# The last four granules of a down projection as one group beside the closing norms, and a sigmoid that stays in its PSUM bank

## The chip, the cores and the metric

The kernel runs on one core of one Trainium2 chip. Its time is the device time of one execution in microseconds; a kernel's time is the median of several executions. PE is the matmul engine, PEld its weight load, DVE, ACT and POOL the three other compute engines, SP the engine on whose queue all the DMAs here are issued.

## The reference

Two blocks on 1024 tokens of 1024 features. The first is a gated mix of attention and convolution, then a two-layer MLP, then a gated product. Only the end of the first block matters here:

```python
h = rms_norm(x, g_pre_mlp[i])
f = jnp.square(jax.nn.relu(h @ w_up[i])) @ w_down[i]
x = x + rms_norm(f, g_post_mlp[i])

ple_gate = jax.nn.sigmoid(rms_norm(x, g_ple[i]) @ w_ple_gate[i])
x = x + ple_gate * (p[i] @ w_ple_proj[i])
```

The hidden width of the MLP is 4096, so the down projection sums over 32 pieces of 128 rows, called granules below. The second block begins with `rms_norm_2(x, norm_pre[0])` and projections of the result.

## The kernel before

All matmuls are done in three passes, because each fp32 operand is split into a high part and a rest: `mm3` (L119) issues high by high (L124), high by rest (L125) and rest by high (L126) for each 128 rows of the sum. A weight is loaded by `split_w` (L90): a DMA into one of two raw buffers (L103), the high part on ACT (L104), the rest on POOL (L105). The two parts go into slots of the pools `w` and `wx`, six slots in all, taken in turn, unless `room` names another pool.

`mlp` keeps the whole result of the down projection in SBUF (`acc`, 8 token tiles by 1024). `down(js)` takes a group of granules: for each token tile t and each half n of the features it sums the group's granules in one PSUM bank (`ps_d`, one of six banks of the tag r) and adds the bank to `acc` on DVE (L1037). There are 16 groups of two granules, so a group has 8 x 2 x 2 x 3 = 96 matmuls and 16 additions to `acc`.

Beside the last group, granules 30 and 31, `after(t)` does the closing work of the token tiles that are complete:

- `final(t)` (L996 to L1017) squares and sums `acc` for tile t and, once the residual is added, for tile t - 1 (L1004 on ACT). Each sum becomes a reciprocal root on DVE in about ten tiny steps (`rstd`, L144 to L163). Tile t is then multiplied by the gain (L1007 on POOL, L1008 on DVE), scaled (L1012 on ACT) and added to the residual `x_f` (L1013 on POOL, L1014 on DVE), and `normed(t - 1)` writes the normed row tile `xn` (L989 on DVE for one half; L991 on ACT and L992 on POOL for the other).
- `turn(t - 3)` transposes `xn` on PE (L183, eight 128x128 transposes into two banks `tp`) and splits it (L112 on ACT, L113 on DVE) into `act_hi` and `act_lo`.
- `ple(n, t - 4)` multiplies by half n of the gate weight (24 matmuls into `ps_pg`), takes the sigmoid on ACT into the SBUF tile `g_p` (L1050), multiplies it by `pp_t` on DVE (L1051) and adds the product to `acc` on POOL (L1052).

After the group, the gate's second half `w1` is loaded (L1069) and `ple(1, t)` runs with the next norm (`leave`) and its transposes. Then come gates of the next layer (`ps_g`, `ps_ad`), whose weights take their slots in the same turn.

In the normed rows, tile 3 has a buffer of its own in the pool `fp` (`xn_f`), and the first two pieces of `w1` lie in that pool too. The order of each engine's instructions is set when the program is built, by a scheduler that works from the program's dependences; on the chip every engine goes through its list in order.

Of the kernel before, what the change touches and what calls it, by code (L numbers as in the profile page):

```python
# [8 lines left out]
F32 = mybir.dt.float32  # L9
# [3 lines left out]
AF = mybir.ActivationFunctionType  # L13
ALU = mybir.AluOpType
# [4 lines left out]
P = 128  # L19
S = 1024  # L20
D = 1024
# [7 lines left out]
class Net:  # L29
# [914 lines left out]
    def mlp(self):  # L944


        nc, tc, a = self.nc, self.tc, self.a
# [4 lines left out]
        with ExitStack() as st:  # L952
# [6 lines left out]
            fp = st.enter_context(tc.tile_pool(name="fp", bufs=2))  # L959
# [3 lines left out]
            f3 = st.enter_context(tc.tile_pool(name="f3", bufs=2))  # L963
            acc = ac.tile([P, NT, D], F32, name="acc")

            def gain(src):
                g = gl.tile([P, D], F32, name="gain", tag="gain")
                nc.sync.dma_start(out=g, in_=src.broadcast_to([P, D]))
                return g

            def load_f(j):

                s = (j + 4) % 8
                fs[j] = hi[:, s, :], lo[:, s, :]
                for h in range(2):
                    sl = slice(h * H, h * H + H)
                    raw = fr.tile([P, H], F32, name="f_raw")
                    nc.sync.dma_start(out=raw, in_=self.fd[j, :, sl])
                    self.split(*(x[:, sl] for x in fs[j]), raw)

            gp, gn = gain(a["g_post_mlp"]), gain(a["g_ple"])

            def normed(t, q, g):
                if t == 3 and g is gn:
                    o = xn[t] = fp.tile([P, D], F32, name="xn_f", tag="fh")
                else:
                    o = xn[t] = f3.tile([P, D], F32, name="xn", bufs=3)
                x = acc[:, t, :]
                nc.vector.scalar_tensor_tensor(out=o[:, :H], in0=x[:, :H], scalar=q, in1=g[:, :H],  # L989
                                               op0=ALU.mult, op1=ALU.mult)  # L990
                nc.scalar.activation(out=o[:, H:], in_=x[:, H:], func=AF.Copy, scale=q)  # L991
                nc.gpsimd.tensor_tensor(out=o[:, H:], in0=o[:, H:], in1=g[:, H:], op=ALU.mult)  # L992
# [3 lines left out]
            def final(t):  # L996

                if t < NT:
                    x = f3.tile([P, D], F32, name="x_f", bufs=1)
                    nc.sync.dma_start(out=x, in_=self.xd[t * P:(t + 1) * P, :])  # L1000
                    a0, a1 = acc[:, t, :H], acc[:, t, H:]
                    ss = self.sm.tile([P, 2 if t else 1], F32, name="ss")
                    for i in range(2 if t else 1):
                        nc.scalar.activation(out=junk(), in_=acc[:, t - i, :], func=AF.Square, accum_out=ss[:, i:i + 1])  # L1004
                    qs = self.rstd(ss, D)
                    q1, q = qs[:, 0:1], qs[:, 1:2] if t else None
                    nc.gpsimd.tensor_tensor(out=a0, in0=a0, in1=gp[:, :H], op=ALU.mult)  # L1007
                    nc.vector.tensor_tensor(out=a1, in0=a1, in1=gp[:, H:], op=ALU.mult)  # L1008
                else:
                    q = self.rstd(self.sumsq(acc[:, t - 1, :], junk()), D)  # L1010
                if t < NT:
                    nc.scalar.activation(out=a0, in_=a0, func=AF.Copy, scale=q1)  # L1012
                    nc.gpsimd.tensor_tensor(out=a0, in0=a0, in1=x[:, :H], op=ALU.add)  # L1013
                    nc.vector.scalar_tensor_tensor(out=a1, in0=a1, scalar=q1, in1=x[:, H:], op0=ALU.mult, op1=ALU.add)  # L1014
                if t:
                    normed(t - 1, q, gn)

            xn = {}

            def turn(t):  # L1020
                self.transpose_split(xn[t], pst, t, hi, lo, 8, 0)

            def down(js, after=None):
                ws = [self.split_w(a["w_down"][j], 1024) for j in js]
                for j in js:
                    load_f(j)
                for t in range(NT):
                    ts = slice(t * P, (t + 1) * P)
                    for n in range(2):
                        sl = slice(n * H, n * H + H)  # L1030
                        ps = psm.tile([P, H], F32, name="ps_d", tag="r")
                        self.mm3(ps, [((fs[j][0][:, ts], fs[j][1][:, ts]), (w[0][:, sl], w[1][:, sl]))
                                      for j, w in zip(js, ws)])
                        if js[0] == 0:
                            nc.vector.tensor_copy(out=acc[:, t, sl], in_=ps)
                        else:
                            nc.vector.tensor_tensor(out=acc[:, t, sl], in0=ps, in1=acc[:, t, sl], op=ALU.add)  # L1037
                    if after is not None:
                        after(t)

            def ple(n, t, ws):
                ts = slice(t * P, (t + 1) * P)
                sl = slice(n * H, n * H + H)
                ps = psm.tile([P, H], F32, name="ps_pg", tag="r")
                self.mm3(ps, [((hi[:, k, ts], lo[:, k, ts]),
                               tuple(w[:, (k % 2) * H:(k % 2) * H + H] for w in ws[k // 2])) for k in range(8)])
                g = f2.tile([P, H], F32, name="g_p", tag="rl")
                pp = f3.tile([P, H], F32, name="pp_t", bufs=1)
                nc.sync.dma_start(out=pp, in_=self.pp[ts, sl])
                nc.scalar.activation(out=g, in_=ps, func=AF.Sigmoid)  # L1050
                nc.vector.tensor_tensor(out=g, in0=g, in1=pp, op=ALU.mult)  # L1051
                nc.gpsimd.tensor_tensor(out=acc[:, t, sl], in0=acc[:, t, sl], in1=g, op=ALU.add)  # L1052

            for c in range(0, 30, 2):
                down([c, c + 1])
            wg = []

            def after(t):
                final(t)
                if t == 0:  # L1060
                    wg.extend(self.split_w(a["w_ple_gate"][0, k], 1024) for k in range(4))
                if t > 2:
                    turn(t - 3)
                if t > 3:
                    ple(0, t - 4, wg)

            down([30, 31], after)
            g0 = gain(a["norm_pre_2"][0:1])
            w1 = [self.split_w(a["w_ple_gate"][1, k], 1024, room=(fp, "fh", "fl") if k < 2 else None) for k in range(4)]  # L1069

            def leave(t):
                if t < NT:
                    ple(1, t, w1)
                    nc.sync.dma_start(out=self.xd[t * P:(t + 1) * P, :], in_=acc[:, t, :])
                if t:
                    normed(t - 1, self.rstd(self.sumsq(acc[:, t - 1, :], junk()), D), g0)

            final(NT)
            turn(NT - 3)
            ple(0, NT - 4, wg)  # L1080
            turn(NT - 2)
            ple(0, NT - 3, wg)
# [13 lines left out]
            for m in range(2):  # L1096
                ps = psm.tile([P, H], F32, name="ps_g", tag="r")
                self.proj_T(ps, self.g01[m], col, act, 8, 0)
                g = f2.tile([P, H], F32, name="g_p", tag="rl")
# [566 lines left out]
```

## Time and profile before

| what | us |
|---|---|
| three executions | 2941.45, 2939.25, 2936.12 |
| median | 2939.25 |
| the profiled execution | 2939.78 |
| its span, first to last instruction | 2938.0 |

The span is cut into busy time by engine and into stretches (windows). A wait is the idle time of an engine with what ended it. In a timeline the bracket behind a row gives the idle time before that row. PE's own rows overlap, since matmuls are pipelined: a 128x512 matmul shows 0.39 us and the next begins 0.23 us later. [...]

### The profile page before, as it was taken

Reading aid. Unit: us, or ns where it says so; the run is one execution under the profiler, and the core shown is the slowest. Engines: PE = TensorE matmul, PEld = TensorE weight load, DVE = VectorE, ACT = ScalarE, POOL = GpSimd, SP = SyncE. Lnnn points to the kernel's source line nnn. Section 1 sums busy time; section 2 is a strip of 40 time slices with the busy share of each in tenths; the row PEclk is TensorE's granted clock in tenths of the full one; section 3 lists DMA queues with packets and bytes.
Section 4 is the critical chain, followed back from the end, with each engine's and each line's share of the span. In section 5 each row is a group of like instructions: output and inputs, shape, how many; then the busy total and the mean of one; then the engine's idle time right before and its main releaser. Section 6 shows DMA issues by size and latency. Waiting matters only on the chain. (4 is left out here: it accounts for less than half of the span.)

```text
span 2938.0 us, 37990 instructions
## 1 busy us (share of the span) xinstructions
PE 2767.0 (94%) x13490; PEld 2303.1 (78%) x13490; DVE 1684.0 (57%) x3177; ACT 1222.8 (42%) x2403; POOL 985.6 (34%) x826
## 2 busy tenths in 40 slices
PE   7999999997999999999989899699999999999988
PEld 5888778886887887888867789677777988788867
DVE  5420288855387766766577534377872436666643
ACT  5111266643352222211134423377773535555542
POOL 4211111113235543222246312332324344555441
PEclk9999999998999999999999999899999999999999
DMA  5112211117323335332123321543344332222163
GB/s 208 47 43 68 75 46 60 58 61 251 118 97 106 128 109 170 115 105 93 66 71 136 133 94 64 180 122 95 121 137 170 106 117 65 72 72 74 56 204 118
DMA packets 140293, 311.15 MB, mean 106 GB/s; under 512 B 15868, under 2 KB 35964, under 8 KB 140104
## 3 DMA queue, kind: packets, MB, share of 16 engines
q1 hardware_dynamic: 140104, 308.73, 31.4%
q8 instruction: 107, 1.75, 0.2%
q14 instruction: 82, 0.67, 0.1%
HBM read 213.33 MB, written 85.38 MB: 102 GB/s over the span
## 5 line engine op out<-in xcount | busy, mean ns | idle before, releaser
L105 POOL TENSOR_TENSOR w_lo<-w_raw,w_hi 128x1024 fp32r<-128x1024 f32 (+5 forms) x223 | 440.2, 1983 | 1036.0 <-ACT w_hi L104 1021.5
L104 ACT ACTIVATE w_hi<-w_raw 128x1024 fp32r<-128x1024 f32 (+5 forms) x223 | 193.0, 877 | 407.3 <-PE ps L125 90.6
L124 PE MATMUL ps_m<-act_hi,w_hi 128*128 128x512 f32 x716 | 287.2, 401 | 22.6 <-DVE qb L343 6.3
L125 PE MATMUL ps_m<-act_lo,w_hi 128*128 128x512 f32 x716 | 281.4, 393 | 0.0
L126 PE MATMUL ps_m<-act_hi,w_lo 128*128 128x512 f32 x716 | 280.7, 393 | 0.2
L113 DVE TENSOR_TENSOR pl<-tp_at,ph 128x512 fp32r<-128x512 f32 (+3 forms) x416 | 222.9, 561 | 84.0 <-ACT ph L112 81.8
L112 ACT ACTIVATE ph<-tp_at 128x512 fp32r<-128x512 f32 (+3 forms) x416 | 196.7, 500 | 107.6 <-PE tp_at L304 96.4
L304 PE MATMUL tp_at<-ident,p 128*128 128x128 f32 x1280 | 204.9, 275 | 18.0 <-DVE pl L113 6.5
L259 ACT ACTIVATE p<-p,mx 128x256 f32<-128x256 f32 (+7 forms) x256 | 180.2, 706 | 74.5 <-DVE mx L248 41.6
L1037 DVE TENSOR_TENSOR acc<-ps_d,acc 128x512 f32<-128x512 f32 x240 | 161.5, 687 | 82.1 <-PE ps_d L126 82.1
L124 PE MATMUL ps_d<-w_hi,act_hi 128*128 128x512 f32 x512 | 200.3, 391 | 2.8 <-DVE f_out L890 1.3
L125 PE MATMUL ps_d<-w_lo,act_hi 128*128 128x512 f32 x512 | 199.5, 390 | 0.0
L126 PE MATMUL ps_d<-w_hi,act_lo 128*128 128x512 f32 x512 | 199.5, 390 | 0.0
L304 PEld LDWEIGHTS tp_at<-ident,p 128*128 128x128 f32 x1280 | 152.6, 141 | 50.6 <-DVE pl L113 9.2
L124 PEld LDWEIGHTS ps_m<-act_hi,w_hi 128*128 128x128 f32 x716 | 135.3, 189 | 58.3 <-PE s_ps L226 8.8
L760 PE MATMUL r_o<-w_hi,act_hi 128*128 128x512 f32 x384 | 152.0, 399 | 12.4 <-DVE ga L692 8.0
L126 PEld LDWEIGHTS ps_m<-act_hi,w_lo 128*128 128x128 f32 x716 | 134.7, 188 | 29.3 <-POOL w_lo L105 1.3
L125 PEld LDWEIGHTS ps_m<-act_lo,w_hi 128*128 128x128 f32 x716 | 135.3, 189 | 25.5
L296 PE MATMUL o_ps<-ph,v 128*128 128x512 f32 (+3 forms) x400 | 146.5, 367 | 6.3 <-ACT ph L112 3.3
L762 PE MATMUL r_o<-w_hi,act_lo 128*128 128x512 f32 x384 | 151.9, 396 | 0.0
L761 PE MATMUL r_o<-w_lo,act_hi 128*128 128x512 f32 x384 | 151.6, 396 | 0.0
L297 PE MATMUL o_ps<-pl,v 128*128 128x512 f32 (+3 forms) x400 | 147.6, 377 | 0.4 <-DVE pl L113 0.2
(393 smaller groups left out, 6930.1 us busy)
## 6 DMA issues: line engine op xcount, KB each, us to landing
w_raw<-in_w_in SPq DMA_DIRECT2D x40, 512.0 KB, 3.5
w_raw<-in_w_up SPq DMA_DIRECT2D x32, 512.0 KB, 3.6
f_rows_up<-f_out SPq DMA_DIRECT2D x64, 256.0 KB, 2.4
f_raw<-f_rows_up SPq DMA_DIRECT2D x64, 256.0 KB, 2.6
w_raw<-in_w_down SPq DMA_DIRECT2D x32, 512.0 KB, 4.5
xd<-x_o SPq DMA_DIRECT2D x16, 512.0 KB, 2.8
x_o<-xd SPq DMA_DIRECT2D x16, 512.0 KB, 10.6
w_raw<-in_w_out SPq DMA_DIRECT2D x13, 512.0 KB, 5.2
```

Of the source, the lines that this page charges most:

```text
L104: nc.scalar.activation(out=hi[:, sl], in_=raw, func=AF.Copy)
L105: nc.gpsimd.tensor_tensor(out=lo[:, sl], in0=raw, in1=hi[:, sl].bitcast(F32), op=ALU.subtract)
L112: nc.scalar.activation(out=hi, in_=src, func=AF.Copy)
L113: nc.vector.tensor_tensor(out=lo, in0=src, in1=hi.bitcast(F32), op=ALU.subtract)
L124: nc.tensor.matmul(out, lhsT=sh, rhs=mh, start=(i == 0), stop=False)
L125: nc.tensor.matmul(out, lhsT=sh, rhs=ml, start=False, stop=False)
L126: nc.tensor.matmul(out, lhsT=sl, rhs=mh, start=False, stop=(i == n - 1))
L259: nc.scalar.activation(out=p[:, :nk], in_=p[:, :nk], func=AF.Exp, scale=-1.0, bias=mx[:, 0:1], accum_out=it["sum"][:, j:j + 1])
L304: nc.tensor.transpose(tp[:, j * P:(j + 1) * P], it["p"][j][:, k * P:(k + 1) * P], self.ident)
L760: nc.tensor.matmul(r, lhsT=a, rhs=wh, start=(k == 0), stop=False)
L762: nc.tensor.matmul(r, lhsT=b, rhs=wh, start=False, stop=(k == 7))
L1037: nc.vector.tensor_tensor(out=acc[:, t, sl], in0=ps, in1=acc[:, t, sl], op=ALU.add)
```

## The change

The last four granules, 28 to 31, form one group of 192 matmuls, so a bank sums four granules and `acc` is added to once for the four. The first two pieces of the gate's first half stay in the six slots and the other two go to the pool `fp`; all four pieces of `w1` go to the six slots. Tile 3's normed rows use the common three buffers. The sigmoid writes its own PSUM bank, and DVE reads that bank. Lines behind L984 move up by three, behind L1066 by two.

```diff
             def normed(t, q, g):
-                if t == 3 and g is gn:
-                    o = xn[t] = fp.tile([P, D], F32, name="xn_f", tag="fh")
-                else:
-                    o = xn[t] = f3.tile([P, D], F32, name="xn", bufs=3)
+                o = xn[t] = f3.tile([P, D], F32, name="xn", bufs=3)
...
-                nc.scalar.activation(out=g, in_=ps, func=AF.Sigmoid)
-                nc.vector.tensor_tensor(out=g, in0=g, in1=pp, op=ALU.mult)
+                nc.scalar.activation(out=ps, in_=ps, func=AF.Sigmoid)
+                nc.vector.tensor_tensor(out=g, in0=ps, in1=pp, op=ALU.mult)
...
-            for c in range(0, 30, 2):
+            for c in range(0, 28, 2):
...
-                    wg.extend(self.split_w(a["w_ple_gate"][0, k], 1024) for k in range(4))
+                    wg.extend(self.split_w(a["w_ple_gate"][0, k], 1024, room=(fp, "fh", "fl") if k > 1 else None)
+                              for k in range(4))
...
-            down([30, 31], after)
+            down([28, 29, 30, 31], after)
...
-            w1 = [self.split_w(a["w_ple_gate"][1, k], 1024, room=(fp, "fh", "fl") if k < 2 else None) for k in range(4)]
+            w1 = [self.split_w(a["w_ple_gate"][1, k], 1024) for k in range(4)]
```

On PE, the place of the first transposes (`tp_...`, of tile 0) among the down projection's matmuls. Before, they stand behind the matmuls of tile 4 in the last group of two (96 + 60 `ps_d` matmuls behind the start of granule 28):

```order
L124 MATMUL ps_d_11623<-w_hi_11371,act_hi_83 128x512
L125 MATMUL ps_d_11623<-w_lo_11372,act_hi_83 128x512
L126 MATMUL ps_d_11623<-w_hi_11371,act_lo_84 128x512
L183 MATMUL tp_11601<-ident_63,xn_11501 128x128 x4
L183 MATMUL tp_11608<-ident_63,xn_11501 128x128 x4
L124 MATMUL ps_pg_11677<-w_hi_11433,act_hi_83 128x512
```

Now they stand inside the last bank of tile 4 of the group of four, 118 matmuls behind that start:

```order
L124 MATMUL ps_d_11549<-w_hi_11227,act_hi_83 128x512
L183 MATMUL tp_11521<-ident_63,xn_11397 128x128 x4
L125 MATMUL ps_d_11549<-w_lo_11228,act_hi_83 128x512
L126 MATMUL ps_d_11549<-w_hi_11227,act_lo_84 128x512
L183 MATMUL tp_11528<-ident_63,xn_11397 128x128 x4
L124 MATMUL ps_pg_11609<-w_hi_11317,act_hi_83 128x512
```

All of the tile's own matmuls moved in front of the first gate matmul in both; what changed is that tiles 0 to 4 bring 120 matmuls of one group, where they brought 60.

On POOL, the pieces of `w1` (`w_lo_...` of L105) among the norms. Before, from tile 4's L1013 on, four pieces (the first stands two rows ahead of this place):

```order
L1013 TENSOR_TENSOR acc_9020<-acc_9020,x_f_11724 128x512
L992 TENSOR_TENSOR xn_11752<-xn_11752,gain_9023 128x512
L105 TENSOR_TENSOR w_lo_11996<-w_raw_11997,w_hi_11995 128x1024
L105 TENSOR_TENSOR w_lo_12002<-w_raw_12003,w_hi_12001 128x1024
L1052 TENSOR_TENSOR acc_9020<-acc_9020,g_p_11888 128x512
L1007 TENSOR_TENSOR acc_9020<-acc_9020,gain_9021 128x512
L105 TENSOR_TENSOR w_lo_12008<-w_raw_12009,w_hi_12007 128x1024
L1013 TENSOR_TENSOR acc_9020<-acc_9020,x_f_11817 128x512
```

Now, from tile 6's L1010 (the L1013 of before) on:

```order
L1010 TENSOR_TENSOR acc_9020<-acc_9020,x_f_11773 128x512
L989 TENSOR_TENSOR xn_11801<-xn_11801,gain_9023 128x512
L105 TENSOR_TENSOR w_lo_11958<-w_raw_11959,w_hi_11957 128x1024
L105 TENSOR_TENSOR w_lo_11964<-w_raw_11965,w_hi_11963 128x1024
L1004 TENSOR_TENSOR acc_9020<-acc_9020,gain_9021 128x512
L105 TENSOR_TENSOR w_lo_11970<-w_raw_11971,w_hi_11969 128x1024
L1010 TENSOR_TENSOR acc_9020<-acc_9020,x_f_11878 128x512
L989 TENSOR_TENSOR xn_11906<-xn_11906,gain_9023 128x512
L1049 TENSOR_TENSOR acc_9020<-acc_9020,g_p_11949 128x512
L105 TENSOR_TENSOR w_lo_11976<-w_raw_11977,w_hi_11975 128x1024
```

The four pieces moved behind tile 6's norm: the first three now stand between the normed rows of tiles 5 and 6.

On POOL again, the end of the stage: the rests of the weights for the next layer's gates among the last normed rows. Before, two stand beside the last two additions to `acc`:

```order
L1052 TENSOR_TENSOR acc_9020<-acc_9020,g_p_12578 128x512
L105 TENSOR_TENSOR w_lo_13078<-w_raw_13079,w_hi_13077 128x1024
L1052 TENSOR_TENSOR acc_9020<-acc_9020,g_p_12645 128x512
L105 TENSOR_TENSOR w_lo_13084<-w_raw_13085,w_hi_13083 128x1024
L992 TENSOR_TENSOR xn_12669<-xn_12669,gain_11987 128x512
L992 TENSOR_TENSOR xn_12704<-xn_12704,gain_11987 128x512
```

Now four stand there:

```order
L1049 TENSOR_TENSOR acc_9020<-acc_9020,g_p_12546 128x512
L105 TENSOR_TENSOR w_lo_12922<-w_raw_12923,w_hi_12921 128x1024
L989 TENSOR_TENSOR xn_12570<-xn_12570,gain_11955 128x512
L105 TENSOR_TENSOR w_lo_12928<-w_raw_12929,w_hi_12927 128x1024
L1049 TENSOR_TENSOR acc_9020<-acc_9020,g_p_12613 128x512
L105 TENSOR_TENSOR w_lo_13046<-w_raw_13047,w_hi_13045 128x1024
L989 TENSOR_TENSOR xn_12637<-xn_12637,gain_11955 128x512
L105 TENSOR_TENSOR w_lo_13052<-w_raw_13053,w_hi_13051 128x1024
L989 TENSOR_TENSOR xn_12672<-xn_12672,gain_11955 128x512
```

Two of the four next-layer pieces that stood earlier in the stage moved to its end, since their slots now hold `w1` until the last gate product.

## Rows read from the trace of the kernel before

**Rows 1.** The page's first part: each engine's busy time, share of the span and instructions.

```profile
PE 2767.0 (94%) x13490; PEld 2303.1 (78%) x13490; DVE 1684.0 (57%) x3177; ACT 1222.8 (42%) x2403; POOL 985.6 (34%) x826
```

**Rows 2.** Windows: bounds, length, busy of PE, PEld, DVE, ACT, POOL, clock, DMA, GB/s.

```profile
1440.00:1475.60 35.60, 35.60 (x159) 29.48 (x158) 17.99 (x26) 3.79 (x4) 9.53 (x4) 1.00 0.18 60
1497.48:1566.00 68.52, 50.93 (x216) 40.25 (x217) 58.27 (x118) 36.11 (x60) 44.19 (x27) 0.85 0.31 108
1566.00:1638.90 72.90, 72.19 (x348) 59.23 (x347) 49.31 (x122) 34.39 (x57) 38.98 (x26) 1.00 0.33 122
1638.90:1651.00 12.10, 8.12 (x36) 6.14 (x34) 8.62 (x19) 7.02 (x11) 5.36 (x4) 0.86 0.37 141
```

**Rows 3.** Waits of PE, 1490 to 1660: line, releaser, total us, times, longest.

```profile
PE tp L183 <- DVE act_lo L113: 11.1, 6, 5.8
PE tp L183 <- DVE xn L989: 7.0, 1, 7.0
PE ps_pg L126 <- DVE act_lo L113: 2.6, 2, 2.2
```

**Rows 4.** Timeline of PE: start us, us, line, operation, idle before and releaser.

```profile
1461.96 0.39 PE L124 MATMUL ps_d<-w_hi,act_hi 128*128 128x512 f32 x1
...
1497.09 0.39 PE L126 MATMUL ps_d<-w_hi,act_lo 128*128 128x512 f32 x1
1504.43 1.08 PE L183 MATMUL tp<-ident,xn 128*128 128x128 f32 x4 [6.95 <-DVE xn L989]
...
1516.55 0.60 PE L183 MATMUL tp<-ident,xn 128*128 128x128 f32 x4
1516.90 0.48 PE L125 MATMUL ps_pg<-w_lo,act_hi 128*128 128x512 f32 x1
...
1543.75 1.12 PE L183 MATMUL tp<-ident,xn 128*128 128x128 f32 x4 [5.83 <-DVE act_lo L113]
...
1557.86 0.78 PE L126 MATMUL ps_pg<-w_hi,act_lo 128*128 128x512 f32 x1 [2.19 <-DVE act_lo L113]
```

**Rows 5.** Timeline of DVE: start us, us, line, operation, idle before and releaser.

```profile
1486.64 0.69 DVE L1037 TENSOR_TENSOR acc<-ps_d,acc 128x512 f32<-128x512 f32 x1 [0.67 <-PE ps_d L126]
...
1503.54 0.75 DVE L989 SCALAR_TENSOR_TENSOR xn<-acc,rstd_y,gain 128x512 f32<-128x512 f32 x1
...
1520.40 0.75 DVE L989 SCALAR_TENSOR_TENSOR xn<-acc,rstd_y,gain 128x512 f32<-128x512 f32 x1
...
1542.35 0.75 DVE L989 SCALAR_TENSOR_TENSOR xn<-acc,rstd_y,gain 128x512 f32<-128x512 f32 x1
...
1548.40 2.31 DVE L153 TENSOR_SCALAR rstd_y<-rstd_x 128x2 int32<-128x2 int32 x1
...
1558.58 0.75 DVE L989 SCALAR_TENSOR_TENSOR xn<-acc,rstd_y,gain 128x512 f32<-128x512 f32 x1
```

**Rows 6.** Timeline of POOL.

```profile
1505.37 1.27 POOL L992 TENSOR_TENSOR xn<-xn,gain 128x512 f32<-128x512 f32 x1
...
1545.45 5.24 POOL L105 TENSOR_TENSOR w_lo<-w_raw,w_hi 128x1024 fp32r<-128x1024 f32 x2
...
1553.14 2.39 POOL L105 TENSOR_TENSOR w_lo<-w_raw,w_hi 128x1024 fp32r<-128x1024 f32 x1
```

**Rows 7.** Lines and tiles: duration in ns, least, median and most.

```profile
L1037 DVE TENSOR_TENSOR acc<-ps_d,acc x240: 674/691/692, 1183.6 to 1544.8; 128x512 f32<-128x512 f32 x120
...
L1008 DVE TENSOR_TENSOR acc<-acc,gain x8: 678/688/1073, 1488.7 to 1555.5; 128x512 f32<-128x512 f32 x8
...
L1051 DVE TENSOR_TENSOR g_p<-g_p,pp_t x16: 679/693/2827, 1523.0 to 1637.3; 128x512 f32<-128x512 f32 x16
...
L113 DVE TENSOR_TENSOR act_lo<-tp,act_hi x96: 415/682/693, 20.1 to 2332.9; 128x512 fp32r<-128x512 f32 x80, 128x384 fp32r<-128x384 f32 x8, 128x256 fp32r<-128x256 f32 x8
...
L1050 ACT ACTIVATE g_p<-ps_pg x16: 577/580/609, 1522.4 to 1634.6; 128x512 f32<-128x512 f32 x16
```

**Rows 8.** DMA issues, 1440 to 1650: KB each, median us to landing.

```profile
w_raw<-in_w_ple_gate SPq DMA_DIRECT2D x8, 512.0 KB, 3.4
```

## The prediction

> **What bounds the kernel now.** The page's first part comes first: PE is busy for 94% of the span and DVE for 57% [rows 1], so the first guess is that PE sets the time and that work taken from DVE is worth nothing. The share is an average, so I went to windows [rows 2]. In the steady down projection (1440 to 1475.6) PE is busy all the time at a clock of 1.00. Where the last group runs beside the norms (1497.48 to 1566) PE is busy for 50.93 of 68.52 us at a mean clock of 0.85, and DVE for 58.27. Behind that, up to 1638.9, PE is nearly full again (72.19 of 72.90); then it loses 4 us more. So the change touches the one place near it where PE starves.
>
> The waits say what it starves for [rows 3]: 7.0 us once for the first normed row tile, 11.1 us in six waits before transposes and 2.6 us in two before gate matmuls, both for the rests that DVE writes (L113). All are the chain of norms: sums, the tiny steps of the root, the normed row, the transposes, the split. The timeline shows two of the idle times ahead of transposes, 6.95 and 5.83 us, and one of 2.19 us ahead of a gate matmul [rows 4]. [...]
>
> What that window loses: a matmul at full clock costs (1497.09 - 1461.96) / 155 = 0.227 us, from the first matmul of granule 28 to the 156th [rows 4]. The window holds 216 PE records [rows 2]; 48 are transposes (six row tiles), which take 0.35 us for four [rows 4]. So 168 x 0.227 + 12 x 0.35 = 42.3 us of work lie in 68.5 us: 26 us are lost. A few missing records and refills behind transposes are work too, so I take **25 us**: 17.6 idle, the rest lower clock.
>
> **The change, part by part.** G is the start of granule 28, 1461.96; up to there both programs are alike.
>
> *The group of four.* The matmuls of granules 28 to 31 stay 192 and PE's work stays. Sixteen additions to `acc` go, 16 x 0.69 = 11 us of DVE [rows 7]. They lay in the pair of granules that no norm ran beside, under a full PE, so I cost them at nothing; the cover is the matmuls, and without it DVE would gain those 11 us. What counts is cover: a token tile now brings 24 x 0.227 = 5.4 us of matmuls beside its norm instead of 2.7.
>
> *The first wait.* Before, tile 0's second addition began at 1486.64 and its normed row at 1503.54, 16.9 us later [rows 5]; POOL's half ended at 1505.37 + 1.27 = 1506.64 [rows 6], 20.0 us later. Now tile 0 is complete behind 24 matmuls and the addition begins at G + 5.4 + 0.2, so at an unchanged pace DVE's half is ready at G + 23.3 and POOL's at G + 25.6. The first transposes stand behind 118 matmuls, G + 26.8, the second four about 0.8 us later. The wait goes, with 2 to 3 us to spare; the margin pays for one weight split (2.4 us, [rows 6]) that POOL now does between tiles 0 and 1.
>
> *Tiles 1 to 4.* Normed rows came 8.4 us apart from tile 0 to tile 2 and 11.0 from 2 to 4 [rows 5]. By the new order the transposes of tiles 1 to 4 stand at about G + 35.5, 42.9, 51.4 and 63.1 (35, 29, 34 and 48 matmuls apart plus 0.8 us for eight transposes). At the old pace POOL's halves of tiles 2 and 4 come at G + 42.5 and 64.5: even, or 1 us late. One weight split and several stretched products stood in those old steps, so I take **1 us** given back, 0 to 6 (6 if all four steps take 11.0 us plus what a lowered clock adds).
>
> *The pieces of `w1`.* This is the price of the change. Two of them lay in a free pool; now all four need slots that the last group frees only at its end E, 72 gate matmuls and four turns behind the 192: G + 43.5 + 16.3 + 3.2 = G + 63. POOL splits three of them between the normed rows of tiles 5 and 6. Before, three stood between tiles 4 and 5 (5.24 + 2.39 us, [rows 6]), and that step took 1558.58 - 1542.35 = 16.2 us instead of 8.4 [rows 5]; a root step that writes two columns took 2.31 us while POOL split [rows 5]. The same will happen to tile 6. I reckon its chain from E: tile 7's sums at E + 3.5, a dozen root steps with 7.6 us of blocking to E + 13.5, the normed row and DVE's splits of tile 5, queued behind it, to E + 16, POOL's half at E + 18. PE wants the former at E + 14 (0.8 + 24 matmuls + 0.8 + 30 matmuls) and the latter at E + 15. So PE waits about 4 us, and 2 more go on the clock, as behind the wait of 2.19 [rows 4]: **6 us**. From below 0, if the chain leads by as much as at tile 0; from above 17, if it lags like the step of 16.2 us with a second, ordinary one behind it.
>
> The pieces themselves are in time: raw data lands 3.4 us behind its issue [rows 8], the third piece can be ready at about E + 13 and the fourth at E + 22, and the second gate half needs them at E + 25 and later.
>
> *The end of the stage.* Two splits for the next layer's gates move to the last norms, so four stand there. PE already loses 4 us there (8.12 busy of 12.10, [rows 2]). Each extra split can block a root step for its 2.4 us [rows 6]; one of the two falls in a gap of POOL, and a lengthened wait also lengthens the lowered clock: **3 us**, 0 to 6.
>
> *The sigmoid in PSUM.* Products with both operands in SBUF took 0.69 us at the median but up to 2.83; forms that read PSUM never passed 0.693 us in 240 and 96 cases [rows 7]. The product becomes such a form: some 5 us of stretching over 16 products go from DVE. They help the chain and are in the paces above, so no own term. The sigmoid took 0.58 us into SBUF [rows 7]; no row shows it into PSUM. Between 0.1 us less and 0.2 more, 16 of them are -2 to +3 us of ACT, beside PE; I take 0. The bank is held about 1 us longer, one of six; PE reaches it again six banks on, at least 16 us later.
>
> [...]
>
> *Normed tile 3 in the common buffers.* Its buffer waits for tile 0's transposes, which stand over 20 us ahead of it: nothing.
>
> **Sum.** -25 + 1 + 6 + 3 = **-15 us**. The profiled execution took 2939.78 us, of which 2938.0 is the span; that is 0.5 above the median of 2939.25, so 2924.8 on its own account and **2924.3 us** against the median.
>
> **Rivals.**
>
> 1. *Full cover.* The chain is fast enough everywhere, since DVE is freed of additions and stretched products; only the end costs its 3 us, if that. For it: steps of 8.4 us against the 11.6 us that 48 matmuls and a turn give. Against it: three splits ahead of tile 6. It gives -25 to -22, **2914 to 2917 us**. Chance 0.2.
> 2. *The gain is given back.* The chain stays the bound, tile 6 costs its upper 17 us and the end its 6: -25 + 1 + 17 + 6 = -1, **2938 us**. For it: DVE was busy for 58 of 68.5 us [rows 2]. Against it: the chain now starts 23.3 us behind G instead of 41.6 (1503.54). Milder forms reach to -8. Chance 0.2.
> 3. *PE is the bound and no cover is missing.* [...] In the window the loads fill 40.25 of 68.52 us, against 29.48 of 35.60 in the steady stretch [rows 2], which says that PE starves just there. That leaves it a chance of 0.02, at **2939 us**.
> 4. *Slower.* One mechanism: the DMA queue. It runs in order, and the rows of the fifth gate product (`pp_t`) now stand behind the third and fourth piece of `w1` and a next-layer weight, which waits for POOL to split the third piece. That product stands on DVE in front of the last normed row. If each of two links in that ring falls one step of 16.2 us late [rows 5], PE waits 32 us: -25 + 32 = +7, **2946 us**. It decides if the wait passes 25 us. Against it: the third piece can be split at E + 13, and the product is due at E + 18. Chance 0.06.
> 5. *It doesn't do what it says.* The order has already put the first transposes behind 118 matmuls, so the cover is real; no chance of its own.
>
> **How the numbers follow.** The forecast, -8 to -20, has 0.52; with the rivals' 0.2, 0.2, 0.02 and 0.06 that makes 1. A measurement of this kernel can tell about 0.2%, 6 us, from no change. Faster by more: forecast, full cover and half of rival 2: 0.82. Within: the other half and rival 3, rounded down: 0.11. Slower: 0.07. The range takes in the forecast, full cover with 1 us for an unseen gain (2913) and rival 2 up to its middle and a little beyond (2937).
>
> **What would show it.** Right: the wait of 7.0 us is gone and PE runs unbroken to the first transposes near 1488.7; the last `ps_d` matmul ends near 1525 instead of 1537; what is left is a wait of a few microseconds before tile 6's transposes near 1540, released by L113 or the normed row, with POOL on L105 just ahead; products reading `ps_pg` at 0.69 us throughout. Wrong: a wait still ahead of the first transposes, several waits near 5 us behind E, or PE waiting for a piece of `w1` or DVE for `pp_t`.

## The result

| | us, median | runs | ratio to before, 95% interval |
|---|---|---|---|
| before | 2940.12 (2936.12 to 2941.45) | 4 | |
| the change | 2921.48 (2918.29 to 2924.51) | 4 | 0.9935 [0.9921, 0.9949] |
| the change, a second time (a1_change) | 2926.61 (2919.02 to 2939.65) | 12 | 0.9945 [0.9930, 0.9961] |

The change makes the kernel 18.6 us faster on the first chip; 15 us were forecast. The profiled execution of the change took 2919.34 us, with a span of 2917.6 us.

The page's first part after the change, with the same columns as [rows 1]:

```profile
PE 2757.5 (95%) x13490; PEld 2298.8 (79%) x13490; DVE 1676.3 (57%) x3161; ACT 1221.9 (42%) x2403; POOL 985.2 (34%) x826
```

The shares hardly move. PE has the same 13490 instructions, DVE has 16 additions fewer. What moved is local, so I measure the stage where it lies: from G, the first matmul of granule 28, to A, the first `ps_ad` matmul of the next stage. Between these two every kernel below has the same number of matmuls and transposes. PE's timeline gives both (start us, us, engine, line, operation, idle before and releaser). First the end A of the kernel before, then G and A of the change:

```profile
1650.95 0.73 PE L124 MATMUL ps_ad<-act_hi,w_hi 128*128 128x512 f32 x2
```

```profile
1459.64 0.39 PE L124 MATMUL ps_d<-w_hi,act_hi 128*128 128x512 f32 x1
...
1488.01 0.63 PE L183 MATMUL tp<-ident,xn 128*128 128x128 f32 x4 [1.46 <-DVE xn L986]
...
1490.28 0.65 PE L183 MATMUL tp<-ident,xn 128*128 128x128 f32 x4 [1.18 <-POOL xn L989]
1491.90 0.61 PE L124 MATMUL ps_pg<-w_hi,act_hi 128*128 128x512 f32 x1 [0.97 <-ACT act_hi L112]
...
1539.39 0.63 PE L183 MATMUL tp<-ident,xn 128*128 128x128 f32 x4 [1.49 <-DVE act_lo L113]
...
1548.18 0.80 PE L124 MATMUL ps_pg<-w_hi,act_hi 128*128 128x512 f32 x1 [3.38 <-ACT act_hi L112]
...
1632.52 1.32 PE L183 MATMUL tp<-ident,xn 128*128 128x128 f32 x8 [2.03 <-DVE act_lo L113]
1633.86 0.96 PE L124 MATMUL ps_ad<-act_hi,w_hi 128*128 128x512 f32 x3
```

Before, the stage took 1650.95 - 1461.96 = 189.0 us; now 1633.86 - 1459.64 = 174.2 us: **14.8 us less**, the forecast's 15. The profiled spans differ by 20.4 us; of that, 2.3 lie ahead of G, where both programs are the same, and some 3 behind A. From run to run these two parts vary by more than that: over the twelve traces of this study G lies between 1459.6 and 1465.3, and the time from A to the end of the span between 1281 and 1293 us. The local measure leaves that out.

The two idle times that answer to the 6.95 and 5.83 us of [rows 4] are 1.46 and 1.49 us now. PE's waits from 1440 to 1660 (line, releaser, us in total, times, longest), which answer to [rows 3]:

```profile
PE ps_pg L124 <- ACT act_hi L112: 4.4, 2, 3.4
PE tp L183 <- DVE act_lo L113: 3.5, 2, 2.0
PE tp L183 <- issue: 3.1, 1, 3.1
PE tp L183 <- DVE xn L986: 1.6, 2, 1.5
PE tp L183 <- POOL xn L989: 1.2, 1, 1.2
PE tp L183 <- DVE rstd_x L144: 0.8, 2, 0.4
```

The "issue" of 3.1 us lies behind A. Without it 11.5 us are left of the 22.2 us that PE waited before (20.7 of them in [rows 3], the rest in two smaller rows of that view). Nearly all lie in three clusters: at the first transposes, behind the last down matmul (its end is E, 1530.43), and ahead of A. The windows (columns as in [rows 2]) show what each does to the granted clock of PE, as a share of its full speed:

```profile
1488.00:1495.30 7.30, 5.15 (x19) 3.73 (x20) 5.15 (x16) 3.27 (x6) 4.00 (x3) 0.78 0.21 72
1495.30:1530.43 35.13, 34.55 (x163) 28.05 (x162) 31.27 (x75) 18.94 (x32) 20.43 (x13) 1.00 0.21 76
1539.30:1553.60 14.30, 10.83 (x41) 8.62 (x42) 12.68 (x22) 6.32 (x10) 11.68 (x7) 0.76 0.48 162
...
1621.00:1633.86 12.86, 10.40 (x54) 7.80 (x52) 11.21 (x21) 8.34 (x13) 8.97 (x5) 1.00 0.56 192
```

Between the first two clusters PE is now busy for 34.55 of 35.13 us at 1.00; before, the window of [rows 2] that takes in both long waits had 50.93 busy of 68.52 us at 0.85. Around the first two clusters the clock fell to 0.78 and 0.76. In a1_change it stayed at 1.00 around the first (1488.00 to 1496.50), and a further wait of 1.56 us came at 1506.65; ahead of E the stage took as long (70.7 and 70.8 us). So the lowered clock alone does not explain the time there. The product and the sigmoid by duration (ns, least/median/most), beside [rows 7]:

```profile
L1048 DVE TENSOR_TENSOR g_p<-ps_pg,pp_t x16: 683/692/694, 1509.3 to 1621.0; 128x512 f32<-128x512 f32 x16
```

```profile
L1047 ACT ACTIVATE ps_pg<-ps_pg x16: 577/582/591, 1508.7 to 1617.2; 128x512 f32<-128x512 f32 x16
```

The product no longer stretches (2827 ns before, 694 now), and neither edit costs anything in its own instruction.

### The profile page after: what moved, and what is told of

It is laid out like the page before. It is cut to its first block, busy times and chain, and to the rows that moved or that the text cites. A ratio compares the mean times of both kernels' runs of the same rounds, so it can differ in the third digit from the quotient of the medians.

```text
span 2917.6 us, 37956 instructions
## 1 busy us (share of the span) xinstructions
PE 2757.5 (95%) x13490; PEld 2298.8 (79%) x13490; DVE 1676.3 (57%) x3161; ACT 1221.9 (42%) x2403; POOL 985.2 (34%) x826
## 3 DMA queue, kind: packets, MB, share of 16 engines
q8 instruction: 107, 1.75, 0.3%
## 5 line engine op out<-in xcount | busy, mean ns | idle before, releaser
L105 POOL TENSOR_TENSOR w_lo<-w_raw,w_hi 128x1024 fp32r<-128x1024 f32 (+5 forms) x223 | 439.0, 1978 | 1012.1 <-ACT w_hi L104 1010.5
L113 DVE TENSOR_TENSOR pl<-tp_at,ph 128x512 fp32r<-128x512 f32 (+3 forms) x416 | 222.7, 560 | 85.3 <-ACT ph L112 83.1
L112 ACT ACTIVATE ph<-tp_at 128x512 fp32r<-128x512 f32 (+3 forms) x416 | 196.6, 500 | 109.0 <-PE tp_at L304 96.4
L304 PE MATMUL tp_at<-ident,p 128*128 128x128 f32 x1280 | 205.0, 275 | 16.9 <-DVE pl L113 6.5
L1034 DVE TENSOR_TENSOR acc<-ps_d,acc 128x512 f32<-128x512 f32 x224 | 150.3, 686 | 73.7 <-PE ps_d L126 73.6
```

What stands on the lines that cost most here:

```text
L105: nc.gpsimd.tensor_tensor(out=lo[:, sl], in0=raw, in1=hi[:, sl].bitcast(F32), op=ALU.subtract)
L112: nc.scalar.activation(out=hi, in_=src, func=AF.Copy)
L113: nc.vector.tensor_tensor(out=lo, in0=src, in1=hi.bitcast(F32), op=ALU.subtract)
L304: nc.tensor.transpose(tp[:, j * P:(j + 1) * P], it["p"][j][:, k * P:(k + 1) * P], self.ident)
```

## The experiments

My theory: the gain is cover, 24 matmuls beside each norm instead of 12. Rivals: the 16 additions taken from DVE, or the products that no longer stretch. The moves of the weight pieces and of tile 3's row come with the group, and no run has them without it. Then: what makes each of the three clusters that are left. G to E to A in us, from the traces; the ratio is the recorded one to the kernel before on the same chip (medians of before: 2937.61 to 2944.88 by chip), which differs a little from the quotient of the medians. S is the start of the 300th matmul or transpose ahead of A, counted in PE's timeline (1582.73 before, 1569.87 in the change).

| kernel | G to E | E to A | of it S to A | G to A | ratio, 95% interval |
|---|---|---|---|---|---|
| before | 75.5 | 113.5 | 68.2 | 189.0 | |
| change | 70.8 | 103.4 | 64.0 | 174.2 | 0.9935 [0.9921, 0.9949] |
| a1_change | 70.7 | 102.7 | 64.0 | 173.4 | 0.9945 [0.9930, 0.9961] |
| e1_sigmoid_only | 75.3 | 109.2 | 65.4 | 184.5 | 0.9985 [0.9972, 0.9998] |
| e2_group_only | 70.8 | 102.5 | 64.0 | 173.2 | 0.9946 [0.9929, 0.9963] |
| e3_two_banks | 72.0 | 103.0 | 64.0 | 175.0 | 0.9942 [0.9921, 0.9962] |
| e7_three | 64.9 | 109.9 | 64.0 | 174.8 | 0.9958 [0.9944, 0.9972] |
| e5_wg_early | 64.1 | 103.0 | 64.0 | 167.1 | 0.9923 [0.9907, 0.9938] |
| e4b_w1_hi | 70.8 | 97.0 | 64.0 | 167.8 | 0.9922 [0.9908, 0.9935] |
| e10_w1_dve | 64.1 | 97.9 | 64.0 | 162.0 | 0.9902 [0.9888, 0.9915] |
| e11_w1_g01_dve | 64.2 | 98.7 | 64.4 | 162.8 | 0.9906 [0.9891, 0.9922] |
| e12_late_bare | 70.9 | 99.6 | 61.1 | 170.5 | 0.9945 [0.9932, 0.9959] |

(In e7 fewer gate matmuls, 50 instead of 72, stand ahead of E, so there only S to A and G to A compare. In all the others each part has the same number of matmuls and transposes.)

**The change again.** 

> The changed kernel once more, beside its parts on one chip. Both theories expect the same: 15 to 20 us below the kernel before, and 172 to 176 us from the first matmul of granule 28 to the first ps_ad matmul (189.0 in the trace of before, 174.2 in that of the change).

It came out so: 18.3 us by the medians, 16.2 by the ratio, and 173.4 us.

**The sigmoid alone**, in the kernel before:

```diff
-                nc.scalar.activation(out=g, in_=ps, func=AF.Sigmoid)
-                nc.vector.tensor_tensor(out=g, in0=g, in1=pp, op=ALU.mult)
+                nc.scalar.activation(out=ps, in_=ps, func=AF.Sigmoid)
+                nc.vector.tensor_tensor(out=g, in0=ps, in1=pp, op=ALU.mult)
```

> The kernel before with one edit: the sigmoid stays in its PSUM bank and the product reads it there. Cover theory (the gain comes from 24 matmuls beside each norm instead of 12): the products stop stretching, which gives DVE some 5 us in the stage but not the missing cover, so 0 to 5 us faster than before, and the wait for the first normed row stays at 6 to 8 us. Sigmoid theory (products that no longer stretch behind the split on POOL carry the gain): 12 us faster or more. Both: no product reading ps_pg above 0.70 us.

PE's waits, 1440 to 1660, its two largest rows:

```profile
PE tp L183 <- DVE act_lo L113: 7.8, 2, 5.2
PE tp L183 <- DVE xn L989: 6.9, 1, 6.9
```

4.4 us faster by the ratio, 4.5 in the stage (2.8 of them behind S), and the first wait stays at 6.9. In the order of before the stretched products did cost something. The sigmoid theory asked for 12 and falls.

**The group alone**: the change with the two lines above undone.

> The changed kernel with the sigmoid back in SBUF; the group of four and the moved weight splits stay. Cover theory: 12 to 18 us faster than before, since only some 5 us of DVE time in stretched products come back, most of it where PE has cover. Sigmoid theory: within 5 us of before. The 4 us that the change gained at the end of the stage: if they came from the product in PSUM, the waits before the last three pairs of transposes come back here (about 4 us), if not they stay away.

It is as fast as the change. The products stretch again, by less than before:

```profile
L1048 DVE TENSOR_TENSOR g_p<-g_p,pp_t x16: 675/692/1765, 1515.0 to 1625.7; 128x512 f32<-128x512 f32 x16
```

So the sigmoid's edit is worth some 4 us without the cover and nothing measurable with it. Two parts that are tried alone needn't add up. From S to A it takes 64.0 us with and without the sigmoid's edit, so the waits left there come from something else.

**The additions back**: each half of a token tile in two banks.

```diff
-                        ps = psm.tile([P, H], F32, name="ps_d", tag="r")
-                        self.mm3(ps, [((fs[j][0][:, ts], fs[j][1][:, ts]), (w[0][:, sl], w[1][:, sl]))
-                                      for j, w in zip(js, ws)])
+                        for k in range(0, len(js), 2):
+                            ps = psm.tile([P, H], F32, name="ps_d", tag="r")
+                            self.mm3(ps, [((fs[j][0][:, ts], fs[j][1][:, ts]), (w[0][:, sl], w[1][:, sl]))
+                                          for j, w in zip(js[k:k + 2], ws[k:k + 2])])
...
```

> The changed kernel with the group of four kept, but each token tile's half summed in two banks of two granules, both added to acc: the 16 additions on DVE that the change had removed are back, and now lie beside the norms; the matmuls beside each norm stay 24. Cover theory: most of the gain stays, 8 to 16 us faster than before (each tile's norm gets 1.4 us more of DVE work against 5.4 us of matmuls). Theory that the 11 us of additions taken from DVE are the gain: at most 7 us faster than before.

The gain stays, though 11 us of additions lie beside the norms again. That rival falls, and the term of nothing for the additions holds. (PE's order differs somewhat here too.)

**Three granules**, 18 matmuls beside each norm:

```diff
-            down([28, 29, 30, 31], after)
+            down([28])
+            down([29, 30, 31], after)
```

> The changed kernel with granule 28 summed alone and a last group of three: 18 matmuls beside each norm, between the 12 of before and the 24 of the change; 16 additions on DVE more than the change. By the order the first gate matmul stands 72 matmuls (16.3 us) behind tile 0's last down matmul, against 48 (10.9 us) before and 96 (21.8 us) in the change. Cover theory: the first wait, 7.0 us before, falls to 1 to 2.5 us, and the whole is 8 to 15 us faster than before. Rival, that only cover for the whole chain (about 20 us) counts: the first wait stays at 5 us or more and the gain below 6 us.

PE's timeline at the first transposes:

```profile
1498.92 0.63 PE L183 MATMUL tp<-ident,xn 128*128 128x128 f32 x4 [3.59 <-DVE xn L986]
```

10.8 us by the medians, 12.4 by the ratio, inside the 8 to 15 of the cover theory; the rival, which wanted a wait of 5 us and a gain below 6, falls. The wait fell from 6.95 to 3.59 us and not to the 1 to 2.5 I had stated. The chain from tile 0's last down matmul to DVE's normed row tells why. Before, from G + 108 x 0.227 to 1503.54 [rows 4, 5], it is 17.1 us; here, from 1463.89 + 66 x 0.227 to 1497.02, 18.1, and the normed row itself takes 1.75 us instead of 0.75 [rows 5]: 19.9 us against the 16.3 of 72 matmuls, which is the wait.

Counted to the end of the normed row, chain less cover gives the first wait in every order: before 17.8 - 10.9 = 6.9 us (measured 6.95), here 3.6 (3.59), in the change 22.8 - 21.3 = 1.5 (1.46). That is the cover theory in numbers. But less cover did not give a smaller gain in the stage: G to A is 14.2 us shorter here and 14.8 to 15.6 in the change, and the two whole times can't be told apart, since their intervals overlap. With 24 matmuls beside each norm the chain was 2.9 us longer than with 18, which took back a part of the cover; the next experiment looks at why.

**The first cluster.** In the change that chain is 22.0 us long (1459.64 + 24 x 0.227 to 1487.11). POOL's and DVE's timeline of the change show it:

```profile
1468.42 2.41 POOL L105 TENSOR_TENSOR w_lo<-w_raw,w_hi 128x1024 fp32r<-128x1024 f32 x1 [3.32 <-ACT w_hi L104]
...
1472.49 2.39 POOL L105 TENSOR_TENSOR w_lo<-w_raw,w_hi 128x1024 fp32r<-128x1024 f32 x1
```

```profile
1469.49 1.89 DVE L1005 TENSOR_TENSOR acc<-acc,gain 128x512 f32<-128x512 f32 x1
...
1472.77 2.12 DVE L162 TENSOR_TENSOR rstd_u<-rstd_u,rstd_t 128x1 f32<-128x1 f32 x1
...
1475.57 0.16 DVE L162 TENSOR_TENSOR rstd_u<-rstd_u,rstd_t 128x1 f32<-128x1 f32 x1
1475.65 0.68 DVE L1034 TENSOR_TENSOR acc<-ps_d,acc 128x512 f32<-128x512 f32 x1
...
1487.11 0.75 DVE L986 SCALAR_TENSOR_TENSOR xn<-acc,rstd_y,gain 128x512 f32<-128x512 f32 x1
```

A root step of one column (L162), 0.16 us three microseconds later, takes 2.12 and ends with POOL's second split (1472.49 + 2.39 = 1474.88). Behind it on DVE stands tile 1's second addition (1475.65), and tile 0's normed row is made in the step of tile 1.

The chain also starts late, and POOL has no part in that. Tile 0's second addition (1465.28, 0.69 us) ends at 1465.97, but ACT squares and sums the tile only from 1468.25 on. The rounding of the third weight piece stands in front of it in ACT's list and waits for that piece's DMA:

```profile
1467.29 1.06 ACT L104 ACTIVATE w_hi<-w_raw 128x1024 fp32r<-128x1024 f32 x1 [6.07 <-DMA w_raw<-in_w_ple_gate]
1468.25 1.04 ACT L1001 ACTIVATE junk_f<-acc 128x1024 bf16<-128x1024 f32 x1
```

In the kernel before, the sum begins 0.04 us behind the end of the addition (1487.37). The experiment moves both pieces, each with its DMA, its rounding on ACT and its split on POOL, one pair of granules ahead:

```diff
             for c in range(0, 28, 2):
+                if c == 26:
+                    wg23 = [self.split_w(a["w_ple_gate"][0, k], 1024, room=(fp, "fh", "fl")) for k in (2, 3)]
                 down([c, c + 1])
...
-                    wg.extend(self.split_w(a["w_ple_gate"][0, k], 1024, room=(fp, "fh", "fl") if k > 1 else None)
-                              for k in range(4))
+                    wg.extend([self.split_w(a["w_ple_gate"][0, k], 1024) for k in (0, 1)] + wg23)
```

> The changed kernel with the third and fourth piece of the first half's gate weight split one pair of granules earlier, so that POOL splits nothing between tiles 0 and 1 of the last group. The order then puts the first transposes behind 106 matmuls of that group instead of 118 (2.7 us earlier), the first gate matmul stays behind 120. Theory that these two splits, which block DVE's root steps, made the waits left at the first transposes (1.5, 1.2 and 1.0 us, and a lowered clock behind them): the chain of tile 0 is 2.4 to 5 us shorter, the first ps_pg matmul comes at G + 28.5 to 30 instead of G + 32.2, and the stage from G to the first ps_ad matmul gets 2 to 5 us shorter than the 173.4 to 174.2 of the change. Rival, that the chain of tile 0 has that length by itself: the first ps_pg stays at G + 32, the wait ahead of the earlier transposes grows to 4 us or more, and the stage stays within 1 us.

DVE's and PE's timelines of this kernel:

```profile
1480.10 1.78 DVE L986 SCALAR_TENSOR_TENSOR xn<-acc,rstd_y,gain 128x512 f32<-128x512 f32 x1
```

```profile
1484.60 0.60 PE L183 MATMUL tp<-ident,xn 128*128 128x128 f32 x4
```

The chain is 14.1 us (G 1460.57, 24 matmuls), 7.9 less, where 2.4 to 5 had been stated; it now ends ahead of its 18.6 us of cover, and no wait is left, though the transposes come earlier. G to E falls by 6.7 us, also more than the 2 to 5 stated. Of the 7.9 us some 2.3 are ACT's wait (here the sum follows the addition at once) and 2.0 the held root step; the rest I put down to tile 1's additions, which no longer come late. The theory had named the splits on POOL alone, and the edit moves all parts of a piece together, so no run gives the price of each. E to A stays at 103.0: this cluster is independent of the next.

**The second cluster.** Behind E POOL splits `w1`. POOL and DVE of the change:

```profile
1535.70 5.16 POOL L105 TENSOR_TENSOR w_lo<-w_raw,w_hi 128x1024 fp32r<-128x1024 f32 x2
...
1542.84 2.38 POOL L105 TENSOR_TENSOR w_lo<-w_raw,w_hi 128x1024 fp32r<-128x1024 f32 x1 [0.73 <-ACT w_hi L104]
```

```profile
1535.80 2.84 DVE L1005 TENSOR_TENSOR acc<-acc,gain 128x512 f32<-128x512 f32 x1 [0.67 <-ACT junk_f L1001]
...
1538.56 0.68 DVE L113 TENSOR_TENSOR act_lo<-tp,act_hi 128x512 fp32r<-128x512 f32 x1
1539.16 1.73 DVE L144 TENSOR_SCALAR rstd_x<-ss 128x2 f32<-128x2 f32 x1
...
1542.97 2.27 DVE L163 SCALAR_TENSOR_TENSOR rstd_y<-rstd_u,rstd_y 128x2 f32<-128x2 f32 x1
...
1546.93 0.75 DVE L986 SCALAR_TENSOR_TENSOR xn<-acc,rstd_y,gain 128x512 f32<-128x512 f32 x1
```

The 1.49 us end with tile 4's L113 (1538.56), which stands on DVE behind the L1005 that took 2.84. The 3.38 us end with ACT's rounding of tile 5's transposes (L112), which stands in ACT's list behind the scaling of tile 6 and so behind tile 6's root:

```profile
1546.32 0.72 ACT L1009 ACTIVATE acc<-acc,rstd_y 128x512 f32<-128x512 f32 x1 [3.06 <-DVE rstd_y L163]
...
1547.56 0.57 ACT L112 ACTIVATE act_hi<-tp 128x512 fp32r<-128x512 f32 x1
```

The experiment keeps loads and rounding of `w1` and drops the four subtractions on POOL (the function returns the rounded tile twice):

```diff
-            w1 = [self.split_w(a["w_ple_gate"][1, k], 1024) for k in range(4)]
+            w1 = [self.hi_only(a["w_ple_gate"][1, k], 1024) for k in range(4)]
```

> The changed kernel without POOL's four splits of w1: the pieces are loaded and rounded as before, but the rounded part stands in for the rests, so the second half's gate products leave out the rests of that weight; matmuls, DMAs and ACT's work keep their number. Theory that these splits make the waits behind the last down matmul (E): the waits of 1.5 and 3.4 us and the slow clock behind them go, and E to the first ps_ad matmul falls from 102.7 to 103.4 us to 95 to 98. Rival, that tile 7's late sums and the length of the chain make them: E to ps_ad stays above 101.

E to A was 102.7 to 103.4 us and is 97.0 now: the splits cost 5.7 to 6.4 us, the term of 6 in the prediction. The wait of 1.49 is gone, and that of 3.38 is 1.08 in its place:

```profile
1546.93 0.50 PE L134 MATMUL ps_pg<-w_hi,act_hi 128*128 128x512 f32 x1 [1.08 <-ACT act_hi L122]
```

**A kernel that beats both.** What POOL does in 2.4 us while DVE is held up, DVE can do itself. On top of e5:

```diff
-            nc.gpsimd.tensor_tensor(out=lo[:, sl], in0=raw, in1=hi[:, sl].bitcast(F32), op=ALU.subtract)
+            (nc.vector if self.dv else nc.gpsimd).tensor_tensor(out=lo[:, sl], in0=raw, in1=hi[:, sl].bitcast(F32), op=ALU.subtract)
...
+            self.dv = True
             w1 = [self.split_w(a["w_ple_gate"][1, k], 1024) for k in range(4)]
+            self.dv = False
```

> The kernel of e5_wg_early with one more edit: the four rests of w1 are subtracted on DVE instead of POOL (128x1024 each; an estimate of 1.2 to 1.4 us from DVE's 0.69 us for 128x512), the result being the same numbers. Theory that a step of DVE's root waits for the end of the POOL split under way (2.31, 1.21, 2.20 and 2.10 us instead of 0.16 in the trace of e5): these stretched steps go, 4 x 1.3 us of DVE work comes, of which part stands in the chain; E to the first ps_ad matmul falls from 103.0 to 97 to 100.5 us, and the whole is 23 to 28 us faster than the kernel before. Rival, that DVE now pays in its own time what it had waited: E to ps_ad stays at 101.5 or above, and the whole within 2 us of e5.

The subtraction's row on DVE, and PE's waits in the stage (three of six rows):

```profile
L105 DVE TENSOR_TENSOR w_lo<-w_raw,w_hi x4: 1216/1226/1721, 1527.7 to 1536.3; 128x1024 fp32r<-128x1024 f32 x4
```

```profile
PE tp L183 <- DVE act_lo L113: 2.3, 2, 2.0
...
PE tp L183 <- POOL xn L989: 0.5, 1, 0.5
PE tp L183 <- DVE rstd_x L144: 0.4, 1, 0.4
```

E to A is 97.9, 5.1 us less than in e5. The median is 2909.18 us against 2938.89 for before on the same chip: 28.8 us by the ratio, a little above the 23 to 28 stated, 27.0 of them in the stage. PE is now busy nearly throughout, from G to A, at full clock (columns as in [rows 2]):

```profile
1460.61:1622.63 162.02, 158.16 (x754) 129.33 (x752) 123.72 (x284) 82.88 (x135) 89.61 (x56) 1.00 0.35 118
```

Most of what is left there is the third cluster.

**The third cluster.** A first trial put the two splits for `g01` on DVE too (`self.dv` reset two lines further down).

> The kernel of e10_w1_dve with the four splits for the next layer's gate weights (end of the stage) on DVE too. Theory that these splits cost PE nothing: the waits of the last 50 us ahead of the first ps_ad matmul stay at the 2.0 and 0.4 us of every program with the changed order, and the stage from G is within 1 us of e10's. Rival, that they still hold the last norms up: the wait of 2.0 us goes and the stage gets 1.5 to 3 us shorter; or DVE's added time makes it longer by as much.

Its premise was wrong: these two stand near 1570, in the middle of the stage, not at its end, and PE lost nothing there. The waits of 2.0 and 0.4 stayed, but that says nothing about the four splits at the end, which belong to weights split later in the program. The next kernel, built on the change, takes those four away (`bare` is true for them):

```diff
-            nc.gpsimd.tensor_tensor(out=lo[:, sl], in0=raw, in1=hi[:, sl].bitcast(F32), op=ALU.subtract)
-        return hi, lo
+            if not bare:
+                nc.gpsimd.tensor_tensor(out=lo[:, sl], in0=raw, in1=hi[:, sl].bitcast(F32), op=ALU.subtract)
+        return hi, hi if bare else lo
```

> The changed kernel without the four weight splits that POOL does beside the last norms of the stage: those four weights (the first of the next stage) are loaded and rounded, but the rounded part stands in for their rests, so the products with them leave the rests out; two of the last transposes move a few gate matmuls. Theory that the four splits cost PE nothing there, though they stretch DVE's normed rows to 2.85 us: E to the first ps_ad matmul stays within 1 us of the 102.7 to 103.4 of the change, with waits of 2 to 2.5 us in the last 50 us. The prediction's own reading, that each pair of splits there costs some 3 us: E to ps_ad falls to 100 or less and the wait of 2.0 us goes.

PE's waits, 1612 to 1640:

```profile
PE ps_ad L128 <- ACT act_hi L116: 0.3, 1, 0.3
```

Here my theory fell. The wait of 2.0 us goes and E to A is 99.6, 3.1 to 3.9 us less; 2.9 of them lie behind S (61.1 instead of 64.0), where the four splits stand. So the splits do cost some 3 us. The whole is not measurably faster than the change (0.9945, intervals overlapping); 3 us is less than such an interval spans.

## Why the prediction was right

The sum, -15, stands against -14.8 in the stage, but in part by luck. The loss of the window and the price of `w1` were forecast well; two other terms missed by some 7 us each, in opposite directions.

- **Loss of the window, -25: near, 24.** Ahead of E the kernel before takes 75.5 us, and e5, which does not wait there, 64.1: 11.4 lost. From E to S it takes 113.5 - 68.2 = 45.3 us, and e4b 97.0 - 64.0 = 33.0: 12.3 lost. That this is missing cover is shown at the first wait, where chain less cover gives the time in three kernels; e2 and e3 show that it is neither the products nor the additions. How much of the rest comes from the pieces and buffers that moved with the group was not measured. The part on the clock shows in windows of before: the granted clock was 0.50 for 10.2, 6.8 and 3.4 us, from 1499.88, 1540.84 and 1557.91, at the waits of 6.95, 5.83 and 2.19 us.
- **The first wait, at nothing: mis-sized, 6.7 us** (70.8 against 64.1 from G to E). The step that failed is "the wait goes, with 2 to 3 us to spare; the margin pays for one weight split". Two pieces are handled beside the chain of tile 0, not one. ACT's rounding of the first of them delays tile 0's sum by 2.3 us, and POOL's split of the second holds a root step for 2.12 us, which makes tile 1's additions late too. The chain up to the normed row grew from 17.1 to 22.0 us, beyond the 16.9 to 19.3 reckoned with. The sign named for a wrong forecast, a wait still ahead of the first transposes, did appear, and E came at G + 70.8 instead of G + 63 (64.1 in e5).
- **Tiles 1 to 4, +1: in range.** No wait over 0.5 us lies between 1495.30 and E in the change, one of 1.56 in a1_change, none in e5. What they cost is contained in the 6.7 us.
- **The pieces of `w1`, +6: right**, 5.7 to 6.4 us by e4b, and nearly in the way described: POOL's splits, blocked root steps, two waits near 1540 and 1548 (1.49 and 3.38) and a lower clock (0.50 for 6.8 us from 1546.76). The 2 us reckoned for the clock are near what before shows: from 1557.86 on, behind the wait of 2.19, eight steps from matmul to matmul take 3.5 us, 1.7 more than at 0.227. The longer wait came through ACT's list, where the prediction had DVE's.
- **The end of the stage, +3: the wrong sign, -4.2.** From S to A the time fell from 68.2 to 64.0 us, though four splits stand there now instead of two. The splits do cost some 3 us (61.1 without them), but the forecast took the loss of before as 4 us that stay. It was 68.2 - 61.1 = 7.1 us, with a clock of 0.86 among its causes [rows 2], and most of that went. That a longer wait lengthens the lowered clock is not shown throughout: it was 0.50 for 3.4 us at this stage's wait of 3.85 us before (from 1643.24), and for 6.8 at the 3.38 of the change. The sigmoid's edit alone takes 2.8 us off in the order of before (e1: 65.4); the group without it takes off all 4.2 (e2). Why the new order does so stays open.
- **Additions and the sigmoid, no term: right** with the group (e3, e2); the product from PSUM takes 692 ns at the median against 693, the sigmoid into PSUM 582 against 580.

With what was measured the sum is -23.7 + 6.7 + 6.4 - 4.2 = -14.8. It must come out so, as all its parts are taken from one table; what it shows is which terms were off.

Of the rivals, full cover needed both sets of pieces out of the way: e10 reaches 28.8 us, more than the 22 to 25 named. The second did not come: PE's waits from the first transposes to E and behind it stayed short, 3.4 us at most. The third, PE as the bound by its share, falls with e10: at a share of 94% 28.8 us were to be had. The fourth would show as a long wait of PE behind E; the longest is 3.4 us.

## What to carry to other kernels

Where a chain of small steps feeds an engine that idles, reckon chain and cover separately: the wait is what is left of one behind the other. Widen the group of work that runs beside the chain, then look at what stands in the chain's way, on another engine whose work holds its steps up (here POOL's splits) or in front of it in an engine's list, and put that work where the chain does not run, or on the chain's own engine if it is faster there. A total that comes out right can hide terms that are wrong; check each by a run of its own. And try the parts of a change one by one in both directions: the sigmoid in PSUM was worth 4 us alone and nothing beside the group.

## What the hardware showed

That a split on POOL holds up a step of DVE was in [rows 5]; how small a step it may be was new: 128x1 values, 0.16 us, took 2.12. The row at 1538.56 is the other side: a subtraction of 128x512 that reads one operand from PSUM takes its usual 0.68 us under the split that then holds the next step, L144, until it ends (1539.16 + 1.73 = 1540.89; 1535.70 + 5.16 = 1540.86).

The two traces of before and the change have 76 DVE instructions of 128x512 between G and A that began while POOL had at least 0.2 us of a `tensor_tensor` left. The 58 that read one operand from PSUM (L113, the additions of banks to `acc`, the products from `ps_pg`) took 0.67 to 0.69 us. The 18 with all operands in SBUF (the multiplications by the gain, the products from `g_p`, the normed rows) took 0.85 to 2.86.

Not every small step is held. In the same stretch of the same two traces 19 `tensor_scalar` steps of 128x1 began while POOL had at least 0.2 us of a `tensor_tensor` left, and none took more than 0.16 us. Of 128x2 there were 17; each ended together with POOL's instruction, after 1.2 us at the median. So the one-column root of tile 0 offers fewer steps to hold than the two-column roots behind it.

The same subtraction of 128x1024 takes DVE 1.23 us at the median and POOL 2.4. Four of them on DVE cost the stage 5.1 us less than on POOL, although DVE was the engine that PE waited for.
